# The down weights of a SwiGLU layer combined and split beside the gate and up products, kept in DRAM and loaded ready

## The chip, the cores and the metric

The kernel runs on one core of a Trainium2 chip. The metric is the device time of one execution in microseconds, the median over the runs shown. One profiled execution stands behind every duration here.

## The reference

A decoder layer on a sequence of 2048 tokens and a model width of 1024: adaLN modulation, a token mixer (sparse attention beside a gated convolution), a post-norm, and a feed-forward part with a post-norm of its own. The change lies in the feed-forward part alone:

```python
def swiglu(h, w_gate, w_up, w_down):
    return (jax.nn.silu(h @ w_gate) * (h @ w_up)) @ w_down

ff = swiglu(modulate(x, sh2, sc2), w_gate[l], w_up[l], w_down[l])
x = layer_norm(DEEPNORM_ALPHA * x + g2[:, None, :] * ff, ln2_g[l], ln2_b[l])
```

The hidden width (D_FF) is 2816, which is 22 blocks of 128 (NF), or 11 pairs of blocks (NP).

## The kernel before, in words

The three products of the feed-forward part are made by a Strassen-like scheme: each operand is cut into 2 by 2 blocks, seven combinations of its blocks are formed (the program numbers them 1 to 7 and takes them in the order HM = 1, 2, 6, 5, 7, 3, 4), and seven products replace eight. A combination is then split into a high and a low float16 half (`split_w`: ACT casts, DVE takes the rest), and every product is three matmuls of 128 x 512: high by high, high by low, low by high.

**Gate and up products.** A loop over the 11 pairs p, and in it over two groups of 1024 tokens. Each of the 22 groups makes 14 products (gate and up, seven combinations) of 12 matmuls each on TensorE (PE, line 1206). `hidden1` and `hidden2` read them out of the eight PSUM banks on DVE and ACT. `put_g` casts the gated values on ACT (line 1239), takes their low half on POOL (line 1240; for the last group, LASTG, on DVE) and stores them to DRAM (`gg_d`, line 1241). In the second group of a pair, `prep_w` loads the raw gate and up weights of the next pair, combines them on POOL and splits them on ACT (line 215) and DVE (line 216).

**Down product.** A loop over eight token blocks q. For each q and each combination m, `down` multiplies the gated values (tile `gi`, loaded from `gg_d`, line 1497, four buffers) by the prepared down weights (tile `wd_tiles[m, p]`, 77 of them, 11 pairs by 7 combinations): 33 matmuls for each (q, m), line 1502. In the first block, q = 0, the seven combinations are taken side by side in three pieces of the pairs (PIECES: 0 to 4, 4 to 8, 8 to 11), with seven PSUM banks open at once. From q = 1 on all prepared weights stay in SBUF.

**Down weights.** `prep_wd` is a generator: for each pair it loads four raw blocks of 256 KB (`wd`, line 1397), forms the combinations with four operations on POOL (`right`, lines 1104 to 1111), and splits each of the seven into its place in SBUF: 24 tiles in a pool of their own (`wdr`), 8 in the ring of the gate and up weights (`wdw`), 2 in a ring of output buffers (`wdt`), the others in the pool that takes the place of the hidden part (`wdo`). Its first 24 steps are drawn in the program after the first group of the last pair, the others inside `down`, when a product needs them.

**After the product.** For each q the seven banks are added up on DVE (line 1535), and POOL multiplies and adds the residual (`residual`, lines 1488 to 1490, with x loaded from `xn_d`; lines 1546 and 1547), then the second norm follows. The rows of the norms (`l1g`, `l1b`, `l2g`, `l2b`, `g2b`) are loaded in `load_rows`, line 1459.

A scheduler sets the order of the instructions on each engine from the program's order and its own estimates. Transfers are issued by SP, in order: a transfer that waits holds up those behind it. Each transfer reports its end to one of eight counters (DMAHW0 to DMAHW7), which are given out in turn, and it is issued only when the transfer before it on that counter has landed.

## Time and profile before

| | us |
|---|---|
| median of three runs | 2590.02 |
| the three runs | 2584.93, 2590.02, 2590.75 |
| profiled execution, its time | 2585.36 |
| profiled execution, its span | 2583.5 |
| PE busy, of the span | 2335.9 (90%) |
| DVE busy | 1835.4 (71%) |
| ACT busy | 1185.9 (46%) |
| POOL busy | 1184.6 (46%) |
| mean granted TensorE clock, share of full speed | 0.956 |

Busy time counts from the start of an engine's work to its end; matmuls overlap a little. The span runs from the first to the last instruction, the time of an execution is 1.9 us more. Rows give the start of an instruction in us from the start of the span, its length, the engine, the line, and in brackets how long the engine sat idle before it and what it waited for.

### The profile page before, as it was taken

The page shows a single profiled execution, that of the slowest core. Times are in us where ns is not written, and L with a number is a line of the kernel's source. Part 1 is how long each engine was busy: PE and PEld are TensorE (multiplying, and loading weights), DVE is VectorE, ACT ScalarE, POOL GpSimd, SP SyncE. Part 2 cuts the span into 40 slices and gives each one's busy share as a digit, 9 for nine tenths or more (in the row PEclk, how much of TensorE's full clock was granted, in tenths as well). Part 3 has the DMA queues.
Part 4 walks back from the last instruction along what each step waited for, and adds up shares of the span by engine and source line. Part 5 has one row for each costly group of instructions (what it writes and reads, how often), then busy time and mean ns, then how long its engine had stood idle before and what let it go on. Part 6 is the DMA issues. An engine that isn't in the chain of part 4 may idle for free. (4 is left out here: it accounts for less than half of the span.)

```text
span 2583.5 us, 38131 instructions
## 1 busy us (share of the span) xinstructions
PE 2335.9 (90%) x13538; PEld 1126.0 (44%) x13538; DVE 1835.4 (71%) x3649; ACT 1185.9 (46%) x2263; POOL 1184.6 (46%) x960
## 2 busy tenths in 40 slices
PE   6799999996878799889969999999999996999998
PEld 3444444443444355445524444444444442444443
DVE  8998999989999877774377676666666687422223
ACT  3687776546766556667643333233323343110000
POOL 3000000004444655786555665565555664855445
PEclk8899999997988899999989999999999997999999
DMA  7321442433131422331233222222223236444443
GB/s 267 130 101 68 144 136 89 161 132 111 59 108 49 145 80 71 106 115 45 84 116 102 90 86 74 76 72 78 86 75 88 87 106 200 149 138 149 131 134 123
DMA packets 213913, 281.69 MB, mean 109 GB/s; under 512 B 15824, under 2 KB 128848, under 8 KB 212944
## 3 DMA queue, kind: packets, MB, share of 16 engines
q1 hardware_dynamic: 213712, 279.17, 33.9%
q8 instruction: 107, 1.75, 0.3%
q14 instruction: 94, 0.77, 0.1%
HBM read 183.20 MB, written 95.91 MB: 108 GB/s over the span
## 5 line engine op out<-in xcount | busy, mean ns | idle before, releaser
L1206 PE MATMUL f<-h,wwg 128*128 128x512 f16 x1800 | 418.8, 383 | 26.5 <-ACT h L1169 19.9
L896 POOL TENSOR_TENSOR pr<-p,ph 128x512 f16<-128x512 f32 x272 | 330.8, 1233 | 218.1 <-ACT ph L895 160.4
L1206 PE MATMUL f<-h,wwu 128*128 128x512 f16 x1800 | 413.5, 379 | 0.0
L1502 PEld LDWEIGHTS <-gi 128*128 128x128 f16 x1848 | 181.5, 99 | 276.1 <-DMA gi<-gg_d 44.8
L1240 POOL TENSOR_TENSOR go<-g,go 128x512 f16<-128x512 f32 x126 | 169.6, 1356 | 275.2 <-ACT go L1239 235.1
L1206 PEld LDWEIGHTS <-wwu 128*128 128x128 f16 x1848 | 180.8, 98 | 234.4 <-issue 17.3
L1206 PEld LDWEIGHTS <-wwg 128*128 128x128 f16 x1848 | 181.8, 99 | 232.0 <-issue 14.1
L1502 PE MATMUL f<-wdo,gi 128*128 128x512 f16 x1032 | 241.9, 387 | 14.9 <-DMA gi<-gg_d 6.9
L865 DVE CUSTOM_DVE_ANT_0 jk<-m,ua 128x512 bf16<-128x512 f32 (+3 forms) x320 | 193.7, 605 | 71.9 <-PE m L863 56.1
L894 ACT ACTIVATE p<-l 128x512 f32<-128x512 f32 x272 | 157.3, 596 | 91.1 <-PE l L890 82.6
L1239 ACT ACTIVATE go<-g 128x512 f16<-128x512 f32 x132 | 82.4, 627 | 230.7 <-issue 82.8
L447 ACT ACTIVATE r<-xs 128x512 f32<-128x512 f32 (+3 forms) x304 | 153.5, 547 | 59.2 <-PE xs L446 15.4
L895 ACT ACTIVATE ph<-p 128x512 f16<-128x512 f32 x272 | 166.1, 632 | 3.9 <-PE o L908 0.8
L1502 PE MATMUL f<-wdr,gi 128*128 128x512 f16 x576 | 136.8, 386 | 16.7 <-DVE g L1213 8.8
L737 PE MATMUL b<-hi,wch 128*128 128x512 f16 x384 | 146.8, 382 | 0.0
L737 PE MATMUL b<-lo,wch 128*128 128x512 f16 x384 | 146.6, 382 | 0.0
L737 PE MATMUL b<-hi,wcl 128*128 128x512 f16 x384 | 146.3, 381 | 0.0
L908 PE MATMUL o<-vst,pr 128*128 128x65 f16 x1088 | 136.1, 197 | 9.3 <-POOL pr L896 9.1
L906 PE MATMUL o<-vst,ph 128*128 128x65 f16 x1088 | 138.7, 195 | 3.1 <-ACT ph L895 2.0
L863 PE MATMUL m<-k1T,qst 128*128 128x512 f16 (+3 forms) x320 | 109.2, 372 | 35.6 <-DVE mp L865 31.5
L907 PE MATMUL o<-vst,ph 128*128 128x64 f16 x1088 | 138.5, 195 | 0.0
L1469 ACT ACTIVATE frs<-fmv,epsw 128x1 f32<-128x1 f32 x16 | 4.7, 295 | 281.7 <-DVE fmv L1466 281.7
(384 smaller groups left out, 5247.2 us busy)
## 6 DMA issues: line engine op xcount, KB each, us to landing
gg_d<-go SPq DMA_DIRECT2D x154, 256.0 KB, 2.6
gi<-gg_d SPq DMA_DIRECT2D x112, 256.0 KB, 3.0
wa<-in_w_ada SPq DMA_DIRECT2D x64, 256.0 KB, 2.9
wg<-in_wg SPq DMA_DIRECT2D x49, 256.0 KB, 2.9
wu<-in_wu SPq DMA_DIRECT2D x49, 256.0 KB, 3.0
wd<-in_wd SPq DMA_DIRECT2D x44, 256.0 KB, 3.0
gi<-gg_d SPq DMA_DIRECT2D x56, 192.0 KB, 2.8
wa<-in_w_ada SPq DMA_DIRECT2D x16, 512.0 KB, 8.6
```

Source lines behind the costliest of these rows:

```text
L447: S_.activation(r[:, i:i + e], ps[:, 0:e], AF.Relu)
L737: T.matmul(ps, w[:, k, j * P:(j + 1) * P], x[:, k], start=n == 0, stop=n == 3 * KT - 1)
L865: V.tensor_tensor_reduce(jk[:, 0:w], ps[:, 0:w], u[:, j * 512:j * 512 + w], scale=1.0, scalar=-3e38, op0=ALU.add, op1=ALU.max, accum_out=m ...
L894: S_.activation(p32, pl_, AF.Exp, scale=DH ** -0.5)
L895: S_.activation(ph, p32, AF.Copy)
L896: G.tensor_tensor(pr, p32, ph, op=ALU.subtract)
L906: T.matmul(o, lhs, vst[:, kt, 64:129], start=kt == 0 and hh == 0, stop=False)
L907: T.matmul(o[:, 0:64], lhs, vst[:, kt, 0:64], start=False, stop=False)
L908: T.matmul(o, pr[:, hh * P:(hh + 1) * P], vst[:, kt, 64:129], start=False, stop=kt == b and hh == 3)
L1206: T.matmul(ps, w[:, x, k * P:(k + 1) * P], h[:, y, :, k], start=n == 0, stop=n == 11)
L1240: (V if (p, grp) in LASTG else G).tensor_tensor(o[:, :, 1], x4, o[:, :, 0], op=ALU.subtract)
L1502: T.matmul(ps, g[:, p - p0, x], wd_tiles[m, p][:, y], start=p == 0 and n == 0, stop=p == NP - 1 and n == 2)
```

## The change

The seven combinations of each pair's down weights are now made inside the loop of the gate and up products: `prep_wd(p)` is drawn step by step in the first group of pair p + 1 (for the last pair, in its own second group). Each split combination is written into one of the ring's output buffers (`outs`) and stored to a new DRAM tensor `wd_d[m, p]`, 256 KB each, 77 in all. `load_wd` loads them back into SBUF in the order in which the first block q = 0 uses them: 24 where the 24 early steps stood, the other 53 before the first product of q = 0. The gated values of q = 0 are loaded over ACT's queue in place of SP's.

```diff
--- before.py
+++ after.py
@@ -157,6 +157,7 @@
     xn_d = [dram(f"xn_d{b}", [P, D], F32) for b in range(NB)]
     h2_d = [dram(f"h2_d{b}", [P, KT * P], F32) for b in range(NB)]
     t_d = {m: dram(f"t_d{m}", [P, 2, 4, CH], F16) for m in HM[3:]}
+    wd_d = {(m, p): dram(f"wd_d{m}_{p}", [P, 2, CH], F16) for m in HM for p in range(NP)}
     g_d2 = [{m: dram(f"gg_d{g}_{m}", [P, 4, NP, 2, P], F16) for m in HM} for g in range(2)]
 
 
@@ -1375,44 +1376,57 @@
     def wd_slots(R):
         for n in range(24):
             yield R.tile([P, 2, CH], F16, name=f"wdr{n}")
+        for n in range(28):
+            yield fo[0].tile([P, 2, CH], F16, name=f"wdo{n}")
         for n in range(8):
             yield wring(f"wdw{n}")
-        for n in range(2):
-            yield outs(f"wdt{n}").rearrange("p a x t -> p (a x t)").rearrange("p (x n) -> p x n", x=2)
-        n = 0
+        n = 28
         while True:
             yield fo[0].tile([P, 2, CH], F16, name=f"wdo{n}")
             n += 1
 
-    def prep_wd():
-
-        R = ff.enter_context(tc.tile_pool(name="fw", bufs=1, side="right", reuse_waits="tile"))
-        gpool[0] = R
-        slots = wd_slots(R)
-        for p in range(NP):
-            b = []
-            for r in range(2):
-                for hh in range(2):
-                    x = raws(f"wd{p}_{r}{hh}")
-                    dma(x, A["wd"][2 * p + r][:, hh * CH:(hh + 1) * CH])
-                    b.append(x)
-            y = sums(f"yd{p}")
-            for m in RIGHT:
-                x = right(G, b, y, m)
-                w = next(slots)
-                split_w(w[:, 0], w[:, 1], x)
-                wd_tiles[m, p] = w
-                yield p
+    def prep_wd(p):
+
+        b = []
+        for r in range(2):
+            for hh in range(2):
+                x = raws(f"wd{p}_{r}{hh}")
+                dma(x, A["wd"][2 * p + r][:, hh * CH:(hh + 1) * CH])
+                b.append(x)
+        yield
+        y = sums(f"yd{p}")
+        for m in RIGHT:
+            x = right(G, b, y, m)
+            w = outs(f"wdp{p}_{m}").rearrange("p a x t -> p (a x t)").rearrange("p (x n) -> p x n", x=2)
+            split_w(w[:, 0], w[:, 1], x)
+            dma(wd_d[m, p], w)
+            yield
+
+    def load_wd():
+        gpool[0] = ff.enter_context(tc.tile_pool(name="fw", bufs=1, side="right", reuse_waits="tile"))
+        slots = wd_slots(gpool[0])
+        for piece in PIECES:
+            for m in HM:
+                for p in range(*piece):
+                    wd_tiles[m, p] = next(slots)
+                    dma(wd_tiles[m, p], wd_d[m, p])
+                    yield
 
     rows = {}
     fo = [None]
     gpool = [None]
-    pwd = prep_wd()
+    PIECES = ((0, 4), (4, 8), (8, 11))
+    pwd = load_wd()
     second = prep_h(1)
     for p in range(NP):
         nxt = {}
         pw = prep_w(p + 1, nxt) if p + 1 < NP else iter(())
         for grp in range(2):
+            pd = iter(())
+            if grp == 0 and p:
+                pd = prep_wd(p - 1)
+            elif grp and p == NP - 1:
+                pd = prep_wd(p)
             if p == 0 and grp == 0:
                 u, v, g11 = heads["u"], heads["v"], heads["g"]
                 gate = temps("gate")
@@ -1426,12 +1440,18 @@
                         if i == 1:
                             next(pw, None)
                         next(pw, None)
+                    if i % 2 == 0:
+                        next(pd, None)
             for i, _ in enumerate(hidden2(fbank, Ws, HT[grp], u, v, g11, p, grp)):
                 if grp == 1 and i % 2 and p:
                     next(pw, None)
+                if i % 2 == 0:
+                    next(pd, None)
                 if p == 0 and grp == 0 and i == 0:
                     for _ in second:
                         pass
+            for _ in pd:
+                pass
             if p == NP - 1 and grp == 0:
                 early_h[0].close()
                 for _ in range(24):
@@ -1490,14 +1510,10 @@
         G.tensor_tensor(x, x, rows["l1b"][hh], op=ALU.add)
         return x
 
-    PIECES = ((0, 4), (4, 8), (8, 11))
-
     def down(q, m, ps, p0, p1_):
         g = gpool[0].tile([P, 4, 2, P], F16, tag="gi", name=f"gi{q}_{m}{p0}", bufs=4)[:, 0:p1_ - p0]
-        dma(g, g_d2[q // 4][m][:, q % 4, p0:p1_])
+        (S_.dma_start if q == 0 else dma)(g, g_d2[q // 4][m][:, q % 4, p0:p1_])
         for p in range(p0, p1_):
-            while (HM[-1], p) not in wd_tiles or (HM[-2], p) not in wd_tiles:
-                next(pwd)
             for n, (x, y) in enumerate(((0, 0), (0, 1), (1, 0))):
                 T.matmul(ps, g[:, p - p0, x], wd_tiles[m, p][:, y], start=p == 0 and n == 0,
                          stop=p == NP - 1 and n == 2)
@@ -1507,6 +1523,8 @@
         banks = {}
         if q == 0:
             banks = {m: fbank() for m in HM}
+            for _ in pwd:
+                pass
             for piece in PIECES:
                 for m in HM:
                     down(q, m, banks[m], *piece)
```

The program's order shows where the scheduler put this. Line numbers are those of each kernel; the names after "waits" are what the instruction waits for (the eight counters, or another engine).

First SP, where the gate and up products end and the down product begins; `gg_d<-go` stores gated values, `wd<-in_wd` loads a raw down weight, `gi` is a load of gated values. Before:

```order
L1241 DMA gg_d_4_396<-go_4_35237 512x1x256 [waits DMAHW6_49,DVE_49]
L1397 DMA wd_10_35497<-in_wd 128x512 [waits DMAHW7_49,DVE_49]
L1497 DMA gi_70_35412<-gg_d_7_369 128x1024 [waits DMAHW0_49,PE_49]
L1459 DMA l1g_35867<-in_ln_g 128x512 [waits DMAHW1_49,DVE_49]
L1241 DMA gg_d_7_390<-go_7_35280 512x1x256 [waits DMAHW2_49,DVE_49]
L1241 DMA gg_d_6_384<-go_6_35276 512x1x256 [waits DMAHW3_49,DVE_49]
L1497 DMA gi_30_35426<-gg_d_3_372 128x1024 [waits DMAHW4_49,PE_49]
L1241 DMA gg_d_5_387<-go_5_35285 512x1x256 [waits DMAHW5_49,DVE_49]
L1241 DMA gg_d_2_381<-go_2_35321 512x1x256 [waits DMAHW6_49,DVE_49]
L1397 DMA wd_11_35499<-in_wd 128x512 [waits DMAHW7_49,Pool_49]
L1497 DMA gi_40_35440<-gg_d_4_375 128x1024 [waits DMAHW0_49,PE_49]
L1397 DMA wd_00_35530<-in_wd 128x512 [waits DMAHW1_49,DVE_49]
```

And in the changed kernel, the last stores of the gate and up part, with the first loads of prepared weights:

```order
L1402 DMA wd_d_10_585<-wdp_4_35906 128x1024 [waits DMAHW6_49,DVE_49]
L1242 DMA gg_d_2_612<-go_2_35925 512x1x256 [waits DMAHW0_49,DVE_49]
L1242 DMA gg_d_3_624<-go_3_35930 512x1x256 [waits DMAHW2_49,DVE_49]
L1402 DMA wd_d_10_552<-wdp_3_35934 128x1024 [waits DMAHW4_49,DVE_49]
L1412 DMA wdo_35950<-wd_d_0_555 128x1024 [waits DMAHW6_49]
L1412 DMA wdo_35952<-wd_d_1_558 128x1024 [waits DMAHW7_49]
L1412 DMA wdo_35954<-wd_d_2_561 128x1024 [waits DMAHW0_49]
L1412 DMA wdo_35956<-wd_d_3_564 128x1024 [waits DMAHW1_49]
L1412 DMA wdo_35958<-wd_d_4_369 128x1024 [waits DMAHW2_49]
L1412 DMA wdo_35960<-wd_d_5_372 128x1024 [waits DMAHW4_49]
L1412 DMA wdo_35962<-wd_d_6_375 128x1024 [waits DMAHW5_49]
L1412 DMA wdo_35964<-wd_d_7_378 128x1024 [waits DMAHW6_49]
```

Raw loads, which waited for DVE and POOL to free their buffers, have become a run of 45 loads of `wdo` that wait for counters and, in three places, for PE. The counter of `wdo_35950` is 6; number 5, the one before it, went to a load of gated values on ACT.

Second ACT at the same place; `go` is the cast of a gated value, `wdo` and `wdp` are casts of down weights, `gi` the loads of gated values of q = 0. Before:

```order
L215 ACTIVATE wdo_35506<-yd_35501 128x512 [waits Pool_49]
L215 ACTIVATE wdo_35517<-wd_10_35497 128x512 [waits DMAHW7_49]
L215 ACTIVATE wdo_35524<-wd_11_35499 128x512 [waits DMAHW7_49]
L215 ACTIVATE wdo_35539<-wd_00_35530 128x512 [waits DMAHW1_49]
L215 ACTIVATE wdo_35510<-wd_01_35495 128x512 [waits Pool_49]
L215 ACTIVATE wdo_35514<-wd_00_35493 128x512 [waits Pool_49]
L215 ACTIVATE wdo_35521<-wd_10_35497 128x512 [waits Pool_49]
```

In the changed kernel:

```order
L1515 DMA gi_70_36112<-gg_d_7_600 128x1024 [waits DMAHW7_49,PE_49]
L1240 ACTIVATE go_2_35925<-g_4_35888 128x4x128 [waits DMAHW0_49,DVE_49,Activation_49]
L1515 DMA gi_30_36126<-gg_d_3_603 128x1024 [waits DMAHW1_49,PE_49]
L1240 ACTIVATE go_3_35930<-g_4_35888 128x4x128 [waits DVE_49,Activation_49]
L216 ACTIVATE wdp_3_35934<-wd_11_35665 128x512 [waits DMAHW3_49,Activation_49]
L1515 DMA gi_40_36140<-gg_d_4_606 128x1024 [waits PE_49]
L1515 DMA gi_14_36154<-gg_d_1_588 128x1024 [waits DMAHW5_49,PE_49]
L1515 DMA gi_24_36168<-gg_d_2_591 128x1024 [waits DMAHW7_49,DMAHW3_49,PE_49]
L1515 DMA gi_64_36182<-gg_d_6_594 128x1024 [waits DMAHW1_49,PE_49]
```

The casts of down weights behind the last group are gone, and 17 loads of gated values stand on ACT, each waiting for PE to have used up an earlier buffer. Between them are the casts `go_2`, `go_3` and `wdp_3`.

The last of these loads, on ACT:

```order
L1515 DMA gi_18_36252<-gg_d_1_588 128x768 [waits DMAHW6_49,DMAHW1_49,PE_49]
L1515 DMA gi_28_36263<-gg_d_2_591 128x768 [waits DMAHW4_49,DMAHW1_49,PE_49]
L1515 DMA gi_68_36274<-gg_d_6_594 128x768 [waits DMAHW7_49,PE_49]
L1515 DMA gi_58_36285<-gg_d_5_597 128x768 [waits DMAHW5_49,PE_49]
L1515 DMA gi_78_36296<-gg_d_7_600 128x768 [waits DMAHW6_49,PE_49]
```

and SP's rows from which their counters come, the last prepared weights and the rows of the norms:

```order
L1412 DMA wdo_36046<-wd_d_9_549 128x1024 [waits DMAHW5_49]
L1412 DMA wdo_36048<-wd_d_10_552 128x1024 [waits DMAHW6_49]
L1412 DMA wdo_36050<-wd_d_8_579 128x1024 [waits DMAHW7_49]
L1412 DMA wdo_36052<-wd_d_9_582 128x1024 [waits DMAHW0_49]
L1412 DMA wdo_36054<-wd_d_10_585 128x1024 [waits DMAHW2_49]
L1479 DMA l1g_36332<-in_ln_g 128x512 [waits DMAHW3_49]
L1479 DMA l1b_36335<-in_ln_b 128x512 [waits DMAHW4_49]
L1479 DMA l1b_36338<-in_ln_b 128x512 [waits DMAHW5_49]
L1479 DMA l2g_36341<-in_ln_g 128x512 [waits DMAHW6_49]
```

Counters go on in turn over both queues: `wdo_36050` has counter 7 and is the one before `gi_68` on it, and `l1b_36338` has counter 5 and is the one before `gi_58`.

Third DVE in the first group of a pair in the gate and up part (`ch` and `u` read a PSUM bank, `wwu` splits an up weight). Before:

```order
L1215 SCALAR_TENSOR_TENSOR g_4_34068<-g_4_34068,u_1_33793 128x512 [waits DVE_49]
L216 SCALAR_TENSOR_TENSOR wwu_4_34103<-wu_11_33837,wwu_4_34103 128x512 [waits DMAHW2_49,Activation_49]
L1226 TENSOR_TENSOR ch_0_34159<-f,u_0_34115 128x512 [waits PE_49,Activation_49]
L1213 SCALAR_TENSOR_TENSOR g_09_34117<-g_09_34117,ch_0_34159 128x512 [waits Activation_49]
L1226 TENSOR_TENSOR ch_1_34176<-f,u_1_34116 128x512 [waits PE_49]
L1215 SCALAR_TENSOR_TENSOR g_09_34117<-g_09_34117,ch_1_34176 128x512 [waits DVE_49]
L1230 TENSOR_TENSOR u_0_34115<-f,u_0_34115 128x512 [waits PE_49]
L1230 TENSOR_TENSOR u_1_34116<-f,u_1_34116 128x512 [waits PE_49]
```

In the changed kernel:

```order
L217 SCALAR_TENSOR_TENSOR wwu_4_34662<-wu_11_34396,wwu_4_34662 128x512 [waits DMAHW5_49,Activation_49]
L1216 SCALAR_TENSOR_TENSOR g_4_34627<-g_4_34627,u_1_34352 128x512 [waits DVE_49]
L217 SCALAR_TENSOR_TENSOR wdp_5_34800<-wd_01_34693,wdp_5_34800 128x512 [waits DMAHW3_49,DMAHW7_49,DMAHW1_49,Activation_49]
L217 SCALAR_TENSOR_TENSOR wdp_1_34731<-wd_00_34691,wdp_1_34731 128x512 [waits DMAHW4_49,DMAHW0_49,Activation_49]
L1227 TENSOR_TENSOR ch_0_34726<-f,u_0_34674 128x512 [waits PE_49]
L217 SCALAR_TENSOR_TENSOR wdp_7_34766<-yd_34730,wdp_7_34766 128x512 [waits DMAHW2_49,Activation_49,Pool_49]
L1214 SCALAR_TENSOR_TENSOR g_09_34676<-g_09_34676,ch_0_34726 128x512 [waits Activation_49]
L1227 TENSOR_TENSOR ch_1_34748<-f,u_1_34675 128x512 [waits PE_49]
L217 SCALAR_TENSOR_TENSOR wdp_6_34843<-wd_00_34691,wdp_6_34843 128x512 [waits DMAHW4_49,Activation_49]
L1216 SCALAR_TENSOR_TENSOR g_09_34676<-g_09_34676,ch_1_34748 128x512 [waits DVE_49]
```

Four splits of down weights now stand between the reads of the PSUM banks, each waiting for ACT's cast.

## Rows read from the trace of the kernel before

**Rows 1.** Busy time by stretch: groups of the gate and up part, down product from 2115.

```profile
core 0: us, PE busy (x) PEld busy (x) DVE busy (x) ACT busy (x) POOL busy (x), PEclk, DMA share, GB/s
1433.00:1505.00 72.00, 72.00 (x335) 32.63 (x334) 48.62 (x58) 22.82 (x41) 41.38 (x30) 1.00 0.26 79
...
2079.00:2115.00 36.00, 36.00 (x169) 16.28 (x168) 35.25 (x31) 17.68 (x33) 30.41 (x20) 1.00 0.37 112
2115.00:2210.00 95.00, 64.57 (x229) 24.16 (x228) 71.26 (x86) 36.38 (x63) 49.47 (x33) 0.82 0.51 166
2210.00:2262.00 52.00, 50.81 (x236) 22.85 (x235) 21.85 (x34) 6.37 (x10) 41.41 (x33) 1.00 0.52 159
```

**Rows 2.** PE in order of time, around the first block of the down product.

```profile
2112.82 2.75 PE L1206 MATMUL f<-h,wwu 128*128 128x512 f16 x12
2115.41 4.70 PE L1502 MATMUL f<-wdr,gi 128*128 128x512 f16 x21
...
2135.59 4.16 PE L1502 MATMUL f<-wdr,gi 128*128 128x512 f16 x12 [8.78 <-DVE g L1213]
2143.31 4.02 PE L1502 MATMUL f<-wdr,gi 128*128 128x512 f16 x9 [3.57 <-DMA gi<-gg_d]
...
2209.82 2.75 PE L1502 MATMUL f<-wdr,gi 128*128 128x512 f16 x12
```

**Rows 3.** Who waited for whom, PE, 2070 to 2220: total us, times, longest.

```profile
PE f L1502 <- DMA gi<-gg_d: 13.0, 7, 3.6
PE f L1502 <- DVE g L1213: 8.8, 1, 8.8
PE f L1502 <- DVE wdo L216: 5.6, 9, 1.2
PE f L1502 <- ACT wdo L215: 2.4, 3, 1.1
```

**Rows 4.** The tile wd: ns min/median/max, first and last start; landing in us.

```profile
L1397 SPq DMA_DIRECT2D wd<-in_wd x44: 327/328/579, 2029.9 to 2198.1; - x44
L215 ACT ACTIVATE wdo<-wd x37: 612/629/631, 2144.1 to 2211.7; 128x512 f16<-128x512 f32 x37
...
L216 DVE SCALAR_TENSOR_TENSOR wdr<-wd,wdr x20: 674/1640/1789, 2080.1 to 2117.9; 128x512 f16<-128x512 f32 x20
...
L1109 POOL TENSOR_TENSOR wd<-yd,wd x11: 1583/1600/1743, 2088.3 to 2207.1; 128x512 f32<-128x512 f32 x11
...
DMA to landing us min/median/max: 2.5/3.0/6.8
```

**Rows 5.** Who waited for whom, DVE, 1400 to 2070.

```profile
DVE vh L1233 <- PE f L1206: 36.4, 20, 1.9
```

**Rows 6.** Busy time by stretch at the start; columns as in rows 1.

```profile
10.00:20.00 10.00, 5.08 (x17) 3.19 (x18) 9.61 (x21) 2.74 (x5) 2.45 (x2) 1.00 1.07 364
20.00:30.00 10.00, 8.18 (x42) 4.26 (x40) 9.75 (x20) 3.65 (x7) 3.42 (x3) 1.00 1.08 365
```

**Rows 7.** DMA, 2142 to 2162: packets, then issues with KB and median us to landing.

```profile
DMA packets 4620, 6.31 MB, mean 315 GB/s; under 512 B 385, under 2 KB 1930, under 8 KB 4619
...
wd<-in_wd SPq DMA_DIRECT2D x7, 256.0 KB, 6.2
gi<-gg_d SPq DMA_DIRECT2D x5, 256.0 KB, 5.3
```

**Rows 8.** The page's part 3, whole span: queues, packets, MB, share.

```profile
q1 hardware_dynamic: 213712, 279.17, 33.9%
```

**Rows 9.** The chain that ended last: start, us, what.

```profile
2285.23 14.43 PE f L1502 x66
...
2337.51 14.43 PE f L1502 x66
```

## The prediction

> **What bounds the kernel now.** I first read the busy time by stretch. In the gate and up part PE is busy 72.00 of 72 us at the full granted clock, and still 36.00 of 36 in the last group [rows 1]. Only fewer matmuls or a gap can move that part, and there is no gap. From 2115 to 2210 the same engine is busy 64.57 of 95 us, at a granted clock of 0.82. From 2210 it is back at 50.81 of 52. So what the change can win lies in those 95 us, the first block q = 0 of the down product.
>
> PE in order of time gives its exact length: the first matmul of q = 0 starts at 2115.41, the first of q = 1 at 2209.82 [rows 2]. That is **94.4 us**. What it would cost without waits comes from the row ahead of it: 12 matmuls start at 2112.82 and the next ones at 2115.41, so one takes 0.216 us. A prepared tile takes three (0.65 us), and the 77 tiles 49.9 us. Hence 44.5 us are lost in q = 0. Who waited for whom splits part of it: 13.0 us for loads of gated values, 8.8 for a PSUM bank that DVE had not read yet, 5.6 and 2.4 for the splits of down weights on DVE and ACT, 29.8 in all [rows 3]. The rest is slow matmuls: 12 of them took 4.16 us behind a gap, where 12 took 2.75 ahead of it [rows 2].
>
> The cause stands in the stretch from 2079 to 2115: DVE 35.25 of 36 us [rows 1], with splits of down weights that begin at 2080.1, while the raw loads last until 2198.1 [rows 4].
>
> **The change part by part.** I count from T, the end of the gate and up products (2115.41 before).
>
> *Work in the gate and up part.* Each pair gets 7 casts on ACT (7 x 0.63 us), 7 splits on DVE (7 x 1.64 with POOL beside them, 0.67 without), 4 operations on POOL (4 x 1.6), and on SP 4 loads and 7 stores (11 x 0.33) [rows 4]. In 72 us that is 4.4, 5 to 11.5, 6.4 and 3.6. DVE goes from 48.62 to at most 60.1 of 72, ACT from 22.82 to 27.2, POOL from 41.38 to 47.8 [rows 1]. DVE there waits for PE, not the other way round: 36.4 us before one kind of bank read alone [rows 5]. What is queued behind a split that waits is the next bank read on DVE; who waits for that is PE, with eight banks of 2.6 us each in hand. The stretch from 2079 shows the same work at 20 splits in 36 us without a gap on PE in that stretch [rows 1]. The change does 7 in 72, and 7 in the last 36. Cost of this part: 0, T does not move. Without that cover the price is the 8.8 us of one late bank [rows 3] for each time it happens.
>
> *The splits in the first block.* The waits for splits and for the late bank (16.8 us) go. What is late next is loads.
>
> *The loads.* In place at T are 24 `wdr` and 8 `wdw` tiles, which the program's order puts into the last group. The other 45 stand on SP behind the last store of a split. That split hangs on ACT: its cast stands behind the load `gi_30`, which waits until PE has used up `gi_20`, 8 tiles or 5.2 us after T. Two casts (1.26), the split (0.68) and two issues (0.66) bring the first `wdo` to about T + 8.2. The first 24 tiles keep PE busy until T + 15.6, so that start is in time.
>
> The pace of the stream: at the start, with the queue full, 364 and 365 GB/s [rows 6], or 0.72 us for 262 kB; I take 0.728. In the loaded stretch around 2150 it was 315 GB/s, or 0.83 us [rows 7]; this is the upper bound. I take the first, since there the pieces are whole rows as here, while around 2150 stores in pieces of 512 bytes ran beside them.
>
> The counters then tie the two queues together. On ACT, `gi_68` may leave only when `wdo_36050`, 43rd of the 45, has landed, and `gi_58` only behind the row `l1b_36338`, the third behind all 45. PE needs `gi_68` for tile 62, at T + 40. So the end of q = 0 follows from the stream: ahead of `gi_58` go 45 tiles, 3 rows, 7 whole `gi` and 3 of three quarters, or 57.25 transfers, 41.7 us. With the start at T + 8.6, 1 us of a hole where `wdo_35962` waits on its counter for `gi_14`, and the 2.3 us that an unloaded landing of 3.0 us [rows 4] has over 0.73, `l1b_36338` lands at T + 53.6. The load `gi_58` behind it takes 5.3 us, as `gi` did under load [rows 7]: T + 58.9. Behind it 12 tiles are left, 7.8 us: T + 66.7. For the slow matmuls behind the gaps I add 2 us: two pieces took 4.16 and 4.02 us where 2.75 and 2.1 are normal [rows 2], 1.4 and 1.9 too long; a clock that never fell would make it 0, and all 12 tiles at half speed 7.8. So **q = 0 takes 68.7 in place of 94.4 us, a gain of 25.7**.
>
> The Trainium skill, "DMA: Bandwidth & Descriptors", section "Issuing engines are not separate DMA queues", says that transfers issued by several engines run on the same 16 DMA engines, and that a second issuer saves only its issue time. The kernel before shows one hardware queue alone [rows 8], so no row here tests it. By that rule the ten `gi` stay in the count; without it 9.25 of the 57.25 would drop out, and the gain would be 6.7 us more.
>
> *After the first block.* The next load of q = 1 stands on SP behind a load of x that waits for POOL, which waits for the row `g2b`. That row lands some five transfers behind `l1b_36338`, at T + 58; with two operations on POOL of 1.6 us [rows 4] and a load, q = 1 has its values at about T + 66, just in time. From there the order is nearly the old one: the chain comes round every 52.3 us (2285.23 to 2337.51 [rows 9]), which the change leaves alone. Cost 0, up to 5 if a row lands late.
>
> **Sum.** 2585.4 - 25.7 = 2559.7, I say **2560 us**. It is made against the profiled execution, 4.7 us under the median of the runs shown and among them. A change below about 0.3% (8 us) cannot be told from none here. With 315 GB/s the stream is 5.8 us longer (2565.5), with half speed on the last 12 tiles as well 2571.
>
> **Rivals.**
> - *The loads keep pace with PE* (15%). If the counters do not hold `gi_68` and those behind it, because the stream is past them sooner, PE runs q = 0 in 49.9 us and some 2 of waits, a gain of 42: 2543. For it speaks that 32 tiles lie ready at T; against it that 45 tiles need 33 us of the stream alone, and the counters stand in the program's order.
> - *The stream is slower, or the clock stays low* (15%). Two queues that disturb each other, or the clock of 0.82 of the old stretch [rows 1] kept throughout: 2566 to 2580.
> - *Next to nothing comes of it* (6%). The pace is set by POOL's chain with its loads of x, which already comes round at 52.3 us where PE needs 49.9; if q = 1 waits on SP for POOL, the 25.7 us go back into q = 1 in large part: 2582 to 2590.
> - *Slower* (4%). One mechanism: on DVE a split that waits for ACT's cast, which waits for POOL's combination, holds the bank reads behind it, and PE runs out of banks in every pair. The price is some 2.6 us for each bank that comes late. It decides from 25.7 us over 11 pairs, 2.3 us a pair; at two late banks a pair (57 us) the time would be 2617. For it speaks that a split takes 1640 ns at the median and 674 at best [rows 4], and DVE's four splits at the head of a group. Against it: DVE's share of 83% at most, and the 36.00 of 36 on PE beside 35.25 on DVE.
>
> The Trainium skill, "SBUF — State Buffer", section "Who interferes with whom", speaks against the change here: a DVE instruction with two SBUF inputs, as a split is, fully blocks against a GpSimd instruction that reads SBUF, whichever came first. The 674 and 1640 ns agree. By it every split could cost its longest, 7 x 1.79 = 12.5 us a pair, and POOL as much; DVE would still have 11 of 72 us free, and the 4% stand.
>
> **How the numbers follow.** The forecast (2554 to 2571) has 60%. Range: from the first rival's 2543 to near the end of the second, **2578**, which leaves out a tenth above and a little below. Faster by over 0.3%: 60 + 15 + 15 = 0.90; within 0.3% 0.06; slower 0.04.
>
> **What would show it.** In the profile after: PE busy all of the time until T near 2115; the first row of the down product to the first of q = 1 66 to 72 us apart; in it no wait for DVE or ACT splits, but waits for `gi`, the largest near T + 40 to T + 58; the granted clock of the stretch above 0.82; a second hardware queue of 17 to 21 loads. I am wrong if PE shows gaps before T, if q = 0 ends near T + 52, or if q = 1 begins with a long wait for `gi` behind x.

## The result

| | before | after |
|---|---|---|
| median of the runs, us | 2590.39 (four runs) | 2562.40 (four runs) |
| runs, us | 2584.93 to 2592.74 | 2558.38 to 2567.45 |
| profiled execution, its time and span, us | 2585.36 and 2583.5 | 2567.45 and 2565.7 |

The ratio of the times is 0.9896, with a 95% interval of 0.9872 to 0.9920: 28 us are gone. A second set of runs of the same kernel gave 0.9907 (0.9880 to 0.9934).

**Where the time went.** Busy time by stretch of the changed kernel, with the columns of [rows 1]:

```profile
1433.00:1505.00 72.00, 72.00 (x336) 32.57 (x334) 56.33 (x65) 25.45 (x46) 47.42 (x35) 1.00 0.40 121
2079.00:2115.00 36.00, 36.00 (x169) 16.30 (x167) 22.59 (x31) 11.59 (x21) 18.23 (x14) 1.00 0.94 318
2115.00:2210.00 95.00, 82.01 (x354) 34.64 (x353) 28.91 (x47) 11.00 (x18) 27.47 (x22) 0.96 0.85 288
2210.00:2262.00 52.00, 50.59 (x234) 22.64 (x233) 12.32 (x23) 4.22 (x7) 33.01 (x26) 1.00 0.47 139
```

In 72 us of the gate and up part DVE has 56.33 us of work where it had 48.62, ACT 25.45 for 22.82, POOL 47.42 for 41.38, and PE still 72.00. In the stretch from 2115 to 2210 DVE has 28.91 us where it had 71.26, PE 82.01 where it had 64.57, and the granted clock is 0.96 instead of 0.82.

PE in order of time, from T (the first matmul of the down product) to the first of q = 1, beside [rows 2]:

```profile
2119.03 2.75 PE L1207 MATMUL f<-h,wwu 128*128 128x512 f16 x12
2121.62 15.70 PE L1518 MATMUL f<-wdr,gi 128*128 128x512 f16 x72
2137.16 3.60 PE L1518 MATMUL f<-wdo,gi 128*128 128x512 f16 x15
...
2144.66 0.81 PE L1518 MATMUL f<-wdo,gi 128*128 128x512 f16 x3 [1.11 <-DMA wdo<-wd_d]
...
2162.17 2.76 PE L1518 MATMUL f<-wdw,gi 128*128 128x512 f16 x12 [1.57 <-DMA gi<-gg_d]
2167.60 3.69 PE L1518 MATMUL f<-wdw,gi 128*128 128x512 f16 x9 [2.66 <-DMA gi<-gg_d]
...
2180.93 9.63 PE L1518 MATMUL f<-wdo,gi 128*128 128x512 f16 x36 [2.21 <-DMA gi<-gg_d]
2190.40 2.75 PE L1518 MATMUL f<-wdr,gi 128*128 128x512 f16 x12
```

T is now 2121.62, and q = 0 lasts until 2190.40: **68.8 us**, where it took 94.4. The 72 matmuls on ready tiles run in 15.54 us without a gap. The waits that are left, from 2100 to 2230, answer to [rows 3] (the shortest of the six for `gi`, 0.65 us, already lies in q = 1):

```profile
PE f L1518 <- DMA gi<-gg_d: 10.3, 6, 2.7
PE f L1518 <- DMA wdo<-wd_d: 3.1, 6, 1.1
```

The 16.8 us that [rows 3] puts down to splits and to a late bank are gone. The sum of the two profiled executions: q = 0 gives 25.6 us, the part from q = 1 on costs 1.6 (375.3 for 373.7), the gate and up part gives 1.9 (PE waits for `h` at its head, around 1343 to 1369 us, 22.9 us before and 20.3 after; no down weight is made there yet). And 8.1 us are lost ahead of all that the change touches: the first matmul of the gate and up products on its own banks starts at 1317.38 instead of 1309.30, in a program that is the same up to there. Together -17.8 us, the difference of the spans. In the second set the same kernel had that point at 1309.62, a span of 2554.9 and q = 0 of 68.3 us. So that loss is a spread from run to run and not the change.

### The profile page after: what moved, and what is told of

It reads as the page before. It is cut to its first block, busy times and chain, and to the rows that moved or that the text cites. A ratio compares the mean times of both kernels' runs of the same rounds, so it can differ in the third digit from the quotient of the medians.

```text
span 2565.7 us, 38373 instructions
## 1 busy us (share of the span) xinstructions
PE 2335.3 (91%) x13538; PEld 1129.1 (44%) x13538; DVE 1834.0 (71%) x3649; ACT 1181.4 (46%) x2263; POOL 1184.2 (46%) x960
## 5 line engine op out<-in xcount | busy, mean ns | idle before, releaser
L1241 POOL TENSOR_TENSOR go<-g,go 128x512 f16<-128x512 f32 x126 | 163.8, 1308 | 229.8 <-ACT go L1240 115.1
L1518 PE MATMUL f<-wdo,gi 128*128 128x512 f16 x1080 | 247.4, 381 | 11.1 <-DMA gi<-gg_d 7.8
L1518 PE MATMUL f<-wdr,gi 128*128 128x512 f16 x576 | 131.4, 379 | 5.6 <-DMA gi<-gg_d 4.8
```

The costliest lines, as they stand in the source:

```text
L1241: (V if (p, grp) in LASTG else G).tensor_tensor(o[:, :, 1], x4, o[:, :, 0], op=ALU.subtract)
L1518: T.matmul(ps, g[:, p - p0, x], wd_tiles[m, p][:, y], start=p == 0 and n == 0, stop=p == NP - 1 and n == 2)
```

## The experiments

All twelve runs in one table. "Gate and up" is the time from that first matmul to T, "q = 0" from T to the first matmul of q = 1, "rest" from there to the end of the span; all three in us, from the profiled execution of each. The ratio is to the kernel before, run beside each.

| run | median | ratio to before (95%) | gate and up | q = 0 | rest |
|---|---|---|---|---|---|
| before | 2590.4 | | 806.1 | 94.4 | 373.7 |
| changed kernel | 2562.4 | 0.9896 (0.9872 to 0.9920) | 804.2 | 68.8 | 375.3 |
| e8, the same again | 2563.7 | 0.9907 (0.9880 to 0.9934) | 803.9 | 68.3 | 373.1 |
| e1, values on SP | 2574.9 | 0.9944 (0.9927 to 0.9960) | 805.7 | 80.0 | 374.7 |
| e2, values on POOL | 2565.3 | 0.9901 (0.9876 to 0.9926) | 803.7 | 70.3 | 374.0 |
| e3, before, values on ACT | 2591.9 | 1.0003 (0.9990 to 1.0015) | 804.0 | 98.3 | 374.4 |
| e4, before, added work | 2588.1 | 0.9992 (0.9981 to 1.0004) | 804.5 | 92.2 | 374.9 |
| e5, POOL, x on DVE | 2563.7 | 0.9907 (0.9873 to 0.9942) | 805 | 66.9 | 372.3 |
| e6, e5 and last pair early | 2566.8 | 0.9917 (0.9892 to 0.9943) | 813.8 | 65.2 | 372.1 |
| e7, last pair early | 2570.0 | 0.9925 (0.9899 to 0.9950) | 814.0 | 64.6 | 374.0 |
| e9, rows amid the stream | 2560.7 | 0.9895 (0.9875 to 0.9915) | 805.8 | 66.7 | 372.2 |
| e10, POOL, rows amid, double pace | 2556.7 | 0.9875 (0.9858 to 0.9891) | 804.3 | 63.8 | 372.6 |
| e11, e10 and stores on ACT | 2558.1 | 0.9869 (0.9852 to 0.9885) | 805.5 | 64.7 | 373.4 |
| e12, e11 and x on DVE | 2558.0 | 0.9865 (0.9849 to 0.9882) | 804.2 | 62.2 | 373.1 |

The theory ahead of them: the gain comes from taking the splits and DVE's backlog out of q = 0, the added work is hidden, and the 19 us that q = 0 still has above PE's 49.9 come from the pace of the loads and from gated values that are tied to loads of another queue. The rivals: the queue brings it alone; the added work costs something; what is left is the pace alone.

### Each half by itself: e1, e3, e4

e1 keeps the stored weights and takes the other queue back:

```diff
-        (S_.dma_start if q == 0 else dma)(g, g_d2[q // 4][m][:, q % 4, p0:p1_])
+        dma(g, g_d2[q // 4][m][:, q % 4, p0:p1_])
```

> The changed kernel with one edit: the gated values of q = 0 go back to SP's queue. There gi_14, which PE needs at its tile 28, stands behind all 45 wdo issues. Theory (the two halves of the change need each other; the splits leave q = 0, but the values must not queue behind the stream): the stream starts near T + 8 and SP issues at the pace of the transfers, so gi_14 lands near T + 42 to T + 47, PE then waits some 20 to 25 us in one piece for gi at tile 28, has 49 tiles (32 us) left, and q = 0 takes 74 to 82 us: 2567 to 2576. Rival A (the other queue does not matter, taking the splits out brings all): q = 0 near 69, 2562. Rival B (the queue is what brings the gain): q = 0 back at 90 or more, 2584 or later.

e3 is the kernel before with that line as the change has it, and nothing else.

> The kernel before with the second half of the change alone: the gated values of q = 0 are issued by ACT, the splits stay where they were. Theory: the 13.0 us of waits for gi in q = 0 are not what bounds it; DVE and ACT with their splits are. On ACT the casts of the splits stand in order behind a gi that waits for PE to free its buffer, so waits for splits grow as waits for gi shrink: q = 0 between 90 and 105 us, 2586 to 2600, no gain. Rival B (the queue brings the gain): q = 0 shorter by 8 to 13 us, 2577 to 2582.

e4 is the kernel before with a generator `early_wd`, which does what the new `prep_wd` does (loads, combinations, splits, stores), drawn in the first groups for nine pairs; nothing reads what it stores.

```diff
+            if grp == 0 and 0 < p < NP - 1:
+                pd = early_wd(p - 1)
...
+                    if i % 2 == 0:
+                        next(pd, None)
```

> The kernel before with the added work alone: beside the gate and up products of nine pairs the down weights are also loaded, combined, split and stored in DRAM (as the change does), but nobody reads them; the old down product is kept, so q = 0 has its splits as before. Theory (the added work lies beside PE and costs nothing there): the gate and up part keeps its length, 806 us from its first products after the heads to T, within 3 us, q = 0 stays at 94 us, 2586 to 2594. Rival D (splits that wait on DVE hold bank reads): some 2.3 us or more a pair, 20 us or more over nine pairs, 2610 or later. Rival F (SP's 11 more issues a pair make raw loads late): 3 to 15 us, 2594 to 2605.

e1 on PE, in order of time, and below it on SP:

```profile
2118.29 15.70 PE L1518 MATMUL f<-wdr,gi 128*128 128x512 f16 x72
2133.83 2.75 PE L1518 MATMUL f<-wdo,gi 128*128 128x512 f16 x12
2164.23 18.00 PE L1518 MATMUL f<-wdo,gi 128*128 128x512 f16 x72 [27.64 <-DMA gi<-gg_d]
```

```profile
2129.05 29.37 SPq L1412 DMA_DIRECT2D wdo<-wd_d  x45
2158.83 2.35 SPq L1515 DMA_DIRECT2D gi<-gg_d  x4
```

After 28 tiles (84 matmuls) PE stands for 27.64 us, in one piece: `gi_14` leaves at 2158.83, behind the 45 `wdo`. After it there is hardly a gap, since all weights are there by then. q = 0 takes 80.0 us and the gain is about half, 0.56% instead of 1.04%. Rival A (69 us) and rival B (90 and more) both fall.

e3 on PE, who waited for whom from 2095 to 2240:

```profile
PE f L1502 <- DMA gi<-gg_d: 22.5, 7, 13.0
PE f L1502 <- DVE wdo L216: 8.5, 7, 2.5
PE f L1502 <- ACT wdo L215: 4.8, 6, 1.7
```

The 8.8 us that [rows 3] puts down to a late bank belong to `gi` as well, as the account of the prediction shows below. Counted so, the waits for `gi` are 22.5 us where they were 21.8, those for splits 13.3 where they were 8.0, and q = 0 takes 98.3 us. ACT's queue gave the values no better place while the splits were there: the load behind the longest wait (13.0 us) left ACT at T + 20.2, behind casts that wait for DVE, where it had left SP at T + 16.9. The queue alone brings nothing, the stored weights alone half, both together all of it.

e4 leaves q = 0 at 92.2 us and the gate and up part at 804.5. Its stretch answers to the first of [rows 1]:

```profile
1433.00:1505.00 72.00, 72.00 (x336) 32.64 (x334) 56.14 (x65) 25.50 (x47) 47.41 (x35) 1.00 0.39 121
```

DVE, ACT and POOL carry the same load as in the changed kernel, and the time is 0.9992 of before, with an interval that holds 1. Rivals D (2610) and F (2594 and more) fall: the added work costs nothing that can be measured here, for the nine pairs that e4 covers.

### What is left of q = 0: e2, e5, e9

e2 issues the values of q = 0 from POOL (`G.dma_start` in place of `S_.dma_start` in the line above), whose loads have counters of their own.

> The changed kernel with one edit: the gated values of q = 0 are issued by POOL, whose DMAs use completion counters of their own, so that their issue no longer waits for a wdo or a row on a shared counter, and ACT's last casts no longer stand behind a gi that waits for PE. Theory (what is left of q = 0 above 49.9 us, some 19, comes in good part from the shared counters): gi waits of the last piece shrink, q = 0 takes 55 to 63 us, total 2549 to 2557. Rival C (it is the pace of the stream alone, 57 transfers of 0.68 to 0.73 us, whoever issues): q = 0 stays at 66 to 70 us, 2560 to 2565. Rival E (POOL's issues cost its own work or come late behind its waits for rows): q = 0 over 70, or POOL late in q = 1, 2565 or more.

Who waited for whom on PE, from 2095 to 2240, then POOL in order of time:

```profile
PE f L1518 <- DMA gi<-gg_d: 9.7, 1, 9.7
PE f L1518 <- DMA wdo<-wd_d: 5.7, 8, 1.7
```

```profile
2174.93 1.26 POOL L1509 TENSOR_TENSOR x<-x,l1g 128x512 f32<-128x512 f32 x1 [10.66 <-DVE l1g L1481]
2176.62 2.54 POOL L1510 TENSOR_TENSOR x<-x,l1b 128x512 f32<-128x512 f32 x2 [0.43 <-DVE l1b L1481]
2179.10 1.12 POOL L1515 DMA_DIRECT2D gi<-gg_d  x2
```

The waits for `gi` in q = 0 have become one of 9.7 us, and the middle of q = 0 now waits for `wdo` itself. The one that is left has another cause: POOL works in order, `gi_78` stands behind an operation on x, and that waits for a row which is loaded behind the whole stream. Without the shared counters the values were tied to the rows behind the stream through POOL. q = 0 stays at 70.3 us. The theory's 55 to 63 missed; rival E had the mechanism.

e5 lets DVE do these operations for the first two row blocks (`E = V if b == 0 or b == 4 else G` in `residual`).

> As the run with the gated values of q = 0 on POOL, and in addition the residual of the first two row blocks (x times l1g plus l1b) is computed by DVE, so that no gi on POOL stands behind an operation that waits for a row behind the stream. In the run on POOL the waits for gi of the middle were gone, but gi_78 stood behind such an operation: one wait of 9.7 us, and PE waited 5.7 us for wdo itself. Theory (what is left of q = 0 is an order that ties values to the end of the stream, then the stream itself): the 9.7 go, the 5.7 stay, the last wdo lands near T + 53 and q = 0 takes 58 to 63 us; total 2550 to 2558. Rival C (the stream is the whole of it): q = 0 stays at 67 us or more, 2560 to 2566. Rival G (what q = 0 gains, q = 1 gives back, since POOL or the rows come late there): q = 0 near 60, but new waits of 5 us or more in q = 1, 2560 to 2566.

q = 0 took 66.9 us, between the theory's range and rival C's. The trace names why; PE, then who waited for whom on POOL:

```profile
2187.10 3.48 PE L1519 MATMUL f<-wdo,gi 128*128 128x512 f16 x9 [8.27 <-DMA gi<-gg_d]
```

```profile
POOL z L1565 <- DMA g2b<-g_d: 12.1, 1, 12.1
```

Now the last value, `gi_48`, stands on POOL behind the first operation with the row `g2b`. The tie moved on to the next row.

e9 leaves the values on ACT and loads five of the rows behind the first 28 `wdo`:

```diff
-            for _ in pwd:
-                pass
+            for i, _ in enumerate(pwd):
+                if i == 35:
+                    load_rows(0)
```

> The changed kernel (gated values of q = 0 on ACT) with one edit: five of the rows (l1g, l1b twice, g2b twice) are loaded amid the stream, behind the wdo that are needed by tile 52, and only l2g and l2b behind it. The last gi on ACT share their completion counters with what SP issued last; that now is a wdo of the last piece or an earlier row in place of l1b and l2g. Theory (it is the tie of the last gi to what stands at the stream's end): the ties move up, but the last wdo now come 5 transfers (3.3 us) later, so little is won: q = 0 takes 63 to 68 us, total 2553 to 2563. Rival C (the stream is the whole of it): 68 to 72 us, 2560 to 2567.

q = 0 took 66.7 us, the gain over the changed kernel (2 us) is within the spread of the runs. As expected, little.

### The start of the stream: e6, e7, e10, e11, e12

e7 is the changed kernel with the last pair's weights prepared one group earlier, so that no split stands ahead of the stream on SP; e6 is e5 with the same edit.

```diff
-            elif grp and p == NP - 1:
-                pd = prep_wd(p)
+            elif grp and p == NP - 2:
+                pd = prep_wd(p + 1)
```

> The changed kernel (gated values of q = 0 on ACT) with one edit: the down weights of the last pair are prepared one group earlier. Theory: the stream starts 0.5 to 2 us sooner, at T + 7.5 to T + 9, and q = 0 is shorter by no more than that, 66 to 69 us, since the tie to the end of the stream stays; total within 3 us of the changed kernel, 2559 to 2565. Rival (the splits of the last pair behind T are what holds q = 0): q = 0 at 62 us or less, 2556 or less. Rival D (the second group of the pair before, which has the gate and up weights to prepare as well, cannot take 7 more splits): PE gaps ahead of T, 2568 or more.

> As the run before it, and in addition the down weights of the last pair are prepared one group earlier (beside the second group of the pair before), so that no split stands ahead of the wdo stream on SP. Theory (the start of the stream at T + 9 to T + 12 is what is left): the first wdo leaves at T + 7.5 to T + 9.5, the waits for wdo shrink from 5.7 to 0 to 3 us, q = 0 takes 52 to 59 us; total 2545 to 2555. Rival (the stores of the last gated values hold SP as long as the split did): the start stays at T + 11, q = 0 as in the run before it. Rival G: as there.

Both shorten q = 0 (64.6 and 65.2 us), and both lose about 10 us ahead of T: the gate and up part takes 814 us. Both missed their range for q = 0. In e7 the stream starts 1.5 us sooner, at T + 7.8 as expected, but q = 0 is 4.2 us shorter, more than the shift, and why stays open. In e6 it starts at T + 7.5 and the waits for `wdo` shrink to 2.9 us, as expected, but the last value still comes 8.0 us late. e7, busy time by stretch, and who waited for whom on PE from 1900 to 2131:

```profile
2047.00:2083.00 36.00, 30.70 (x132) 13.00 (x130) 26.91 (x27) 14.58 (x25) 29.15 (x20) 0.91 0.37 118
```

```profile
PE f L1207 <- DVE wwu L217: 3.8, 1, 3.8
PE f L1207 <- ACT wwu L216: 1.5, 1, 1.5
```

The second group of a pair already prepares the gate and up weights of the next pair. With 7 more splits there, the last `wwu` come late, PE stands, and its next matmuls run at a clock of 0.91 on the mean of that stretch. Rival D of e7 named this. With 2570.0 us e7 is 6 us and more above both sets of the changed kernel; its four runs lie above all eight of theirs, though the intervals of the ratios overlap. The added work is free in the first group of a pair and cost some 10 us in the one second group, of the last pair but one, where it was tried.

e10 puts together what the runs before had pointed to: values on POOL, five rows amid the stream, and the last pair's splits at double pace in its own second group, which has no gate and up weights to prepare (`if i % 2 == 0 or grp:` at both places that draw `pd`).

> The changed kernel with three edits: the gated values of q = 0 on POOL; five of the rows amid the stream, so that POOL's operations on rows, behind which the last gi stand, find their rows there; and the down weights of the last pair prepared at double pace in its own second group (which has no gate and up weights to prepare), so that no split stands ahead of the stream on SP. Theory (q = 0 is made of the 49.9 us of PE, the start of the stream, and values tied to its end): first wdo at T + 7.5, no gi wait over 3 us, waits for wdo of 3 to 6 us, q = 0 takes 53 to 60 us, the gate and up part keeps its 804 us; total 2546 to 2556. Rival G (what q = 0 gains, q = 1 gives back at POOL or at the late l2g and l2b): new waits of 5 us or more in q = 1, 2556 to 2564. Rival D (twice the pace makes PE wait ahead of T, as one group earlier did, where the part took 814 us): 2558 or more.

The gate and up part keeps its 804.3 us and q = 0 takes 63.8, above the expected 53 to 60. The start missed: the first `wdo` left at T + 12.3, not T + 7.5, since seven stores of gated values that wait for DVE still stood ahead of it. e11 moves these to ACT:

```diff
-        dma(g_d2[grp][m][:, :, p], o)
+        (S_.dma_start if (p, grp) == (NP - 1, 1) else dma)(g_d2[grp][m][:, :, p], o)
```

> The run before (gated values of q = 0 on POOL, five rows amid the stream, last pair's splits at double pace) with one edit: the stores of the last group's gated values, seven of them, which wait for DVE until T + 12 and stood ahead of the stream on SP, are issued by ACT. Theory (the start of the stream was held by SP's order, not by the buffers): the first wdo leaves at T + 4 to T + 7 instead of T + 12.3, the waits for wdo (5.3 us) go to 0 to 2, the rows amid the stream land sooner and the 4.3 us for gi shrink to 0 to 3; q = 0 takes 51 to 58 us instead of 63.8, total 2544 to 2553. Rival C (the stream is the whole of it): shorter by the shift of its start alone and no more, 57 us or more. Rival G (what q = 0 gains, q = 1 gives back): q = 0 under 58 and new waits of 5 us or more in q = 1.

SP in order of time in e10, then in e11, and who waited for whom on SP in e11 from 2118 to 2160:

```profile
2130.33 21.57 SPq L1412 DMA_DIRECT2D wdo<-wd_d  x28
```

```profile
2122.77 30.25 SPq L1412 DMA_DIRECT2D wdo<-wd_d  x28
```

```profile
SPq L1412 <- DMA gg_d<-go: 11.3, 7, 3.1
SPq L1412 <- DMA wdo<-wd_d: 7.0, 15, 1.1
```

and the busy time of e11 over these 28 issues:

```profile
2122.77:2153.02 30.25, 25.69 (x113) 10.79 (x112) 5.31 (x9) 1.39 (x3) 6.46 (x10) 1.00 0.97 323
```

The stream starts at T + 4.1 (T is 2118.66) as the theory said, but its 28 issues take 30.25 us instead of 21.57. Seven times SP waited for a store on ACT, 11.3 us in all. The weights need nothing from these stores; they share the eight counters with them, and a counter is passed on only when its transfer has landed. The last of the 28 leaves at T + 34.4, in e10 at T + 33.9. So the earlier start won nothing, and q = 0 is 64.7 us. That the counters took it back is not shown: the DMA engines were busy 0.97 of these 30.25 us, where a full stretch of the changed kernel reads 1.05 (2162 to 2172). That leaves, as an estimate, some 2 us of idle DMA for 8.7 us of delay. The stores, which ran ahead of the stream in e10, run beside it here, and their transfers take the time as well. No run separates the two.

e12 adds e5's edit to e11.

> The run before and in addition the residual of the first two row blocks on DVE, so that no gi of the last piece but one stands behind an operation on rows at POOL. Theory: q = 0 at 51 to 55 us, total 2543 to 2552; DVE takes eight operations of 0.7 us in place of POOL, in a stretch where it is idle most of the time. Rival H (DVE waits for a row with bank reads of q = 0 behind it): waits for DVE of 1 to 4 us at the end of q = 0, 2548 to 2558.

62.2 us, above the expected 51 to 55 and yet the shortest q = 0; 2.6 of it are a wait for the first value of q = 1. No wait for DVE (rival H) appeared. The times of e10, e11 and e12 lie within 1.4 us of one another, some 5 us below the changed kernel. Their intervals still overlap with those of both sets of the changed kernel (the second begins at 0.9880, e12's ends at 0.9882), so that they beat it is likely and not shown.

> The changed kernel once more, beside the runs of this set on the same chip. Expected as before: 2558 to 2568, q = 0 of 67 to 70 us; the time T at which the gate and up products end may move by some us from run to run, as 2115.4 and 2121.6 did for a program that is the same up to there.

e8 came out as expected: 68.3 us and 2563.7.

## Why the prediction was right

The forecast was 2560 us, the measured median 2562.4. Point by point:

- **T does not move.** Right: 806.1 us of gate and up products before, 804.2 after, and 804.5 with the work added alone (e4). That there is no gap in this part was said too widely: it holds for the stretches of [rows 1], not for the head of the part, where PE waits for `h`. The change leaves that wait alone. DVE's 56.33 of 72 us lie inside the 53.6 to 60.1 that the sum gave, and a split took what [rows 4] had shown, 675 to 1798 ns. That the profiled T is 6.2 us later comes from ahead of the change. The tile `wdp` in the changed kernel, 1400 to 2122, ns min/median/max:

```profile
L217 DVE SCALAR_TENSOR_TENSOR wdp<-wd,wdp x64: 675/1230/1798, 1409.8 to 2115.3; 128x512 f16<-128x512 f32 x64
```

The rule of the Trainium skill that spoke against the change ("SBUF — State Buffer", "Who interferes with whom") agrees with that spread, and DVE has the room for it; no run here took POOL's work away beside a split.

- **The splits and the late bank leave q = 0.** Right that these waits are gone, but the late bank was misread. In these matmuls the gated values are the weights, which PE loads ahead of the products. PE's weight load of the kernel before, where the 8.78 us of [rows 2] end:

```profile
2135.59 0.13 PEld L1502 LDWEIGHTS <-gi 128*128 128x128 f16 x2 [9.27 <-DMA gi<-gg_d]
```

This load of values had left SP only at 2132.27, behind raw loads that wait for DVE and POOL to free their buffers, and it landed at 2135.55. The DVE instruction that [rows 3] names ended within 0.01 us of that and reads no bank. So of the 29.8 us in [rows 3], 21.8 were late values and 8.0 splits, and DVE's backlog reached PE in good part through SP's order: from 2110 to 2215 SP's raw loads, with the values behind them, stood 36.9 us for DVE's splits. Whether a bank was late too is not shown. The sum did not hang on it, since the forecast of q = 0 was built on the chain of loads; the 8.8 us as the price of a late bank have no row behind them.
- **The chain to the end of q = 0.** Right step by step. The chain that ended last in the changed kernel, from 2160 on:

```profile
2164.50 5.25 DMA wdo<-wd_d
...
2169.77 5.26 DMA l1b<-in_ln_b
2175.03 0.02 issue
2175.06 0.02 ACTq L1515
2175.07 0.04 issue
2175.11 5.78 DMA gi<-gg_d
2180.89 0.05 issue
2180.93 11.14 PE f L1518 x43
```

The row lands at T + 53.4 (forecast 53.6), the value behind it on the shared counter at T + 59.3 (58.9), and 12 tiles later q = 1 starts at T + 68.8 (68.7). Before, the chain of the same stretch ran through raw loads, POOL and splits.

- **The terms in it** were less exact than their sum. SP of the changed kernel in order of time, and who waited for whom on it from 2118 to 2180:

```profile
2130.88 37.19 SPq L1412 DMA_DIRECT2D wdo<-wd_d  x45
```

```profile
SPq L1412 <- DMA gi<-gg_d: 4.1, 3, 3.2
```

The first `wdo` left at T + 9.3, not 8.2, since the cast `go_3` ahead of the last split waited 2.3 us for DVE. The pace was better than 0.728 us: from 2162 to 2172 the DMA engines moved 385 GB/s (0.68 us a transfer), and 45 `wdo` by themselves left in 29.37 us in e1 (0.65 us). And SP stood for `gi` on a shared counter for 4.1 us, not 1. At 0.66 us, a value between the two, 57.25 transfers take 37.8 us instead of 41.7. By this count the 3.9 us saved nearly cancel the 3.1 lost at the counters and the 1.1 lost at the start. The order of the chain was foreseen; that its end came out to 0.4 us is in part luck.

- **The second queue adds no rate.** The DMA from 2132 to 2167, first in the changed kernel, with SP's queue (q1) and ACT's (q10), then in e1, with SP's alone:

```profile
DMA packets 7316, 12.68 MB, mean 362 GB/s; under 512 B 776, under 2 KB 1339, under 8 KB 7314
q1 hardware_dynamic: 6146, 10.61, 84.2%
q10 hardware_dynamic: 1168, 2.05, 17.7%
```

```profile
DMA packets 7339, 13.38 MB, mean 382 GB/s; under 512 B 812, under 2 KB 812, under 8 KB 7338
```

Two queues moved no more than one. Beside ACT's values the 45 `wdo` take 37.19 us to issue instead of 29.37. ACT issued some 8.5 transfers of values meanwhile, 5.5 us of the 7.8 at 0.65; for the rest there are SP's waits for `gi` at shared counters (4.1 us). The rule of the Trainium skill that the prediction named ("DMA: Bandwidth & Descriptors", "Issuing engines are not separate DMA queues") holds here; without it the forecast of the gain would have been 6.7 us larger.
- **Slow matmuls.** The forecast allowed 2 us. The last 36 take 9.47 us until q = 1 where 36 take 7.78, so 1.7:

```profile
2162.00:2172.00 10.00, 6.45 (x21) 2.19 (x21) 0.00 (x0) 0.00 (x0) 0.00 (x0) 0.83 1.05 385
2181.00:2190.50 9.50, 9.50 (x37) 3.97 (x38) 3.96 (x6) 0.00 (x0) 6.28 (x6) 0.82 0.35 105
```

Busy time by stretch, as above: the granted clock is 0.82 in the last one, part of it at 1.2 GHz in place of 2.4, behind a gap. The other slow stretch, at 0.83, is hidden by the next wait.

- **From q = 1 on.** Cost 0 to 5 was said, 1.6 and -0.6 were measured.

The forecast was counted from a profiled execution below the median. In medians the gain is 28.0 us, and 25.0 in the second set, where 25.7 was forecast for q = 0.

Of the rivals, that the loads keep pace (2543) fell to the ties that the forecast named. The stream was not slower and the clock of the old stretch did not stay at 0.82 (it was 0.96), and from q = 1 on no more than 1.6 us was given back. "Slower" fell in the place where the change works, but its kind of mechanism is real: e7 shows it one group earlier, through late `wwu` in place of late banks, at 10 us. In the changed kernel DVE did stand 70.6 us for ACT's casts of `wdp` from 1400 to 2070, up to 4.6 us at a time, and PE waited for no bank.

Where my later theory failed: I took the ties for the larger part of the 19 us that are left, and expected 51 to 63 us without them. Each time that a tie was taken away (e2, e5, e11) another took its place or the stream itself did, and 62.2 was the least. In e10 the last `wdo` leaves at T + 51.6, a `wdo` takes 6.7 us to land there (the median from 2131 to 2165), and one tile stands behind it: T + 59. So, by this estimate, with a stream that starts at T + 12 no more than some 5 of the 63.8 us could still be had. Whether a start at T + 4 with counters of its own would give 55 us was not tried.

## What to carry to other kernels

Work that floods one short stretch can go where its engines have time to spare, through DRAM, if the stretch where it is read has the transfers to spare; but put it into a group that has no other preparation, or its cover is gone. Look at what stands in order ahead of a load, on its queue and on its completion counter: the half of this gain hung on that, and each queue or counter that was freed showed the next one. When a term of a sum cannot be read, follow the chain to its last load: here the chain named the right waits in the right order. That its end was right to 0.4 us, while three of its terms were off by 1 to 4, is no measure of the method. And where two waits end within 0.01 us of each other, look at what the engine's weight loads waited for before naming a cause.

## What the runs showed that I had not expected

- The start of the gate and up products on their own banks lies between 1306.8 and 1318.8 us in the fourteen profiles, for a program that is the same up to there; from there to T the kernels without a late weight agree to 2.4 us. A span of one profile says little about 10 us, the length of a stretch says more. What spreads ahead of it was not looked into.
- Loads on SP's queue waited 11.3 us, in seven waits, for stores on ACT's queue (e11) without any data between them.
- While stores of gated values (pieces of 512 bytes) run, the DMA moves less. The DMA of e10 from 2122 to 2131, with five of these stores issued, and from 2131 to 2165, when they are done; how the loss is shared with the loads beside them is not shown:

```profile
DMA packets 3178, 2.30 MB, mean 256 GB/s; under 512 B 139, under 2 KB 2898, under 8 KB 3177
```

```profile
DMA packets 6938, 13.01 MB, mean 383 GB/s; under 512 B 798, under 2 KB 1310, under 8 KB 6937
```

- POOL takes 0.54 us to issue a load of values (1.12 for two in e2), ACT 0.33.
